# Elimination scratch in other buffers, more yields in it, and four HGRN tiles projected among the delta rule's pairs

## The chip, the cores and the metric

One core of a Trainium2 chip runs the whole kernel. The metric is the device time of one execution in microseconds (us). The kernel before was timed in three runs: median 3533.93 us, from 3527.35 to 3548.31.

## The reference

One decoder layer for 512 tokens of width 2048. Two groups of token mixers read the same normalised input through one projection `W_in`; a second part (PEER, an expert lookup) follows and is not touched.

```python
xn = rmsnorm(h)
a_q, a_f, a_i, a_g, b_q, b_k, b_v, b_z, b_b, b_a = split(xn @ w_in)
# HGRN2, 8 heads: S_t = diag(f_t) S_{t-1} + (1 - f_t) outer v_t;  o_t = S_t^T q_t
# gated delta rule, 8 value heads over 4 key heads, in chunks:
#   M = I + strict_lower(kb k^T * L);  u = M^-1 (v beta);  w = M^-1 (kb exp(gc))
#   v_new = u - w S;  o = (q exp(gc)) S + a_qk v_new;  S = S dl + kd^T v_new
h = h + concat(o_a, o_b) @ w_out
h = h + peer(rmsnorm(h))
```

## The kernel before

**The stream of projections.** `W_in` has 57 tiles of 128 columns. A tile is projected in 16 *steps*; a step (`mm3`) is three TensorE matmuls of 128x512 (high and low halves of weight and input), lines L239 to L241. A weight unit of eight steps is loaded by DMA (SP), its high half is cast on ACT (L100), and the low half is subtracted on POOL (L102); three buffers each. A finished tile gets a follow-up on DVE and ACT: a causal convolution and SiLU for q, k and v of the delta rule (`conv_silu`, L245, L362, L364, L369, tanh on ACT in L367), a gate (`gate`, L245, L285, tanh in L284), or f and K of an HGRN head (`forget`).

**The chains.** Beside that stream run the token mixers, one after the other: four pairs of delta rule heads (`gdn_pair`), then eight HGRN heads (`hgrn_head`). They are written as generators. `run` takes one piece of a chain, up to its `yield`, and then lets the stream go on by 1.8 steps on average in the pairs and by 5 in the HGRN heads. It stops the stream at a tile whose kind has two results waiting already (`self.live[self.coming] > 1`), since each kind has two buffers. `self.jobs()` is the order of the tiles.

**One pair.** Keys are normalised and multiplied (L420), the decays are applied on DVE (L432), and the diagonal 32x32 blocks go to DRAM and back (L435, L492), so that 32 blocks lie on 128 partitions. `substitute` then inverts them on DVE in 31 steps of a product (L498) and a sum (L500):

```python
for s in range(IB - 1):
    w = IB - 1 - s
    m = self.ft("t_sq", bufs=2)[:, 0:8 * IB].rearrange("p (j i) -> p j i", j=8)[:, :, 0:w]
    nc.vector.tensor_tensor(m, nb[...], T_[:, :, s:s + 1].to_broadcast([P, 8, w]), op=ALU.mult)
    nc.vector.tensor_tensor(T_[:, :, s + 1:], T_[:, :, s + 1:], m, op=ALU.add)
    if s % 4 == 3:
        yield
```

The product's buffer `t_sq` is also that of the squares for the norms (L376 on ACT, ahead of the norm's matmul L380). The result goes to DRAM and back (L504, L508), and TensorE combines the blocks to 64 and to 128 (`inverse`, L527 to L545; buffers `iTN` and `iY`, which nothing uses during the elimination). The q tile is normalised beside this (`unit_q`: L376, L380, ACT L151 and L152, DVE L383). Then each of the two heads runs a chain of small matmuls (L557 to L576) and a norm (L144, L145).

A scheduler orders the instructions of each engine ahead of time from the order in which they were written and from what each waits for; on the chip every engine takes its own in that order.

Of the kernel before, what the change touches and what calls it, by code (L numbers as in the profile page):

```python
# [33 lines left out]
IB = 32  # L34
# [43 lines left out]
class Kernel:  # L78
# [131 lines left out]
    def proj_steps(self, jobs):  # L210

        a, b = self.proj(jobs, 0), self.proj(jobs, 1)
        for _ in range(LAG):
            next(a)
            yield
        yield from self.zipped(a, b)
        for i in range(2, len(jobs)):
            yield from self.proj(jobs, i)
# [263 lines left out]
    def substitute(self):  # L482


        nc = self.nc
        TT = self.TT
        nb = self.ft("iN", (P, IB, IB))
        T_ = self.ft("iT", (P, 8, IB))
        nc.sync.dma_start(T_, self.a["eye"])
        yield  # L490
        for g in range(IG):
            nc.sync.dma_start(nb[g * NX:(g + 1) * NX], self.nd.rearrange("j h c s t -> (j h c) s t"))  # L492
        for _ in range(WAIT):
            yield
        for s in range(IB - 1):
            w = IB - 1 - s
            m = self.ft("t_sq", bufs=2)[:, 0:8 * IB].rearrange("p (j i) -> p j i", j=8)[:, :, 0:w]
            nc.vector.tensor_tensor(m, nb[:, s:s + 1, s + 1:].to_broadcast([P, 8, w]),  # L498
                                    T_[:, :, s:s + 1].to_broadcast([P, 8, w]), op=ALU.mult)
            nc.vector.tensor_tensor(T_[:, :, s + 1:], T_[:, :, s + 1:], m, op=ALU.add)  # L500
            if s % 4 == 3:
                yield
        for g in range(IG):
            nc.sync.dma_start(self.td.rearrange("j h c s t -> (j h c) s t")[:, 8 * g:8 * g + 8],  # L504
                              T_[g * NX:(g + 1) * NX])
        for j in range(P // IB):
            sl = slice(j * IB, (j + 1) * IB)
            nc.sync.dma_start(TT[sl, :, :, sl], self.td[j].rearrange("h c s t -> s h c t"))  # L508
        for _ in range(WAIT):
            yield  # L510
# [79 lines left out]
    def forget(self, ps, h):  # L590

        nc = self.nc
        th = self.ft("t_th", bufs=2)
        self.normed(th, ps)
        nc.scalar.activation(th, th, AF.Tanh, scale=0.5)
        F = self.ft("hF", bufs=2)
        nc.vector.tensor_scalar(F, th, self.f_mul[:, h:h + 1], self.f_add[:, h:h + 1], op0=ALU.mult, op1=ALU.add)
        K = self.ft("hK", bufs=2)
        nc.vector.tensor_scalar(K, th, self.k_mul[:, h:h + 1], self.f_mul[:, h:h + 1], op0=ALU.mult, op1=ALU.add)
        return F, K  # L600
# [121 lines left out]
    def jobs(self):  # L722

        key = lambda j: (36 + j, lambda ps: self.conv_silu(ps, 4 + j, "gk"), "k")
        out = [(56, self.gates, "gates")]
        for j in range(4):
            if j == 0:
                out.append(key(0))
            out.append((32 + j, lambda ps, j=j: self.conv_silu(ps, j, "gq"), "q"))
            for h in (2 * j, 2 * j + 1):  # L730
                if j < 3 and h % 2:
                    out.append(key(j + 1))
                out.append((40 + h, lambda ps, h=h: self.conv_silu(ps, 8 + h, "gv"), "v"))
                out.append((48 + h, self.gate, "u"))
        for h in range(8):
            out.append((8 + h, lambda ps, h=h: self.forget(ps, h), "f"))
            out.append((h, lambda ps: self.keep(ps, "hQ"), "r"))
            out.append((16 + h, lambda ps: self.keep(ps, "gv"), "v"))
            out.append((24 + h, self.gate, "u"))
        return out  # L740
# [605 lines left out]
```

## Time and profile before

| | |
|---|---|
| Median of three runs | 3533.93 us |
| The profiled execution | 3537.38 us |
| its span, first to last instruction | 3534.2 us |
| TensorE (PE) busy | 3323.9 us, 94% of the span |
| DVE busy | 2760.3 us, 78% |
| ACT busy | 1206.8 us, 34% |
| POOL busy | 878.8 us, 25% |
| Mean granted TensorE clock | 0.966 |

The first 1100 us or so hold the projections with the delta rule (from about 60 to 545 us), the HGRN heads and the output projection; PEER takes the rest. Busy shares are those of the whole span, and the change lies in its first sixth, so the stretches and waits of that part are what to read.

### The profile page before, as it was taken

To read this page: it belongs to the slowest core of one execution; us is meant where nothing else is said; L and a number is where in the kernel's file an instruction comes from. 1 tells how busy PE (TensorE), PEld (TensorE's weight loads), DVE (VectorE), ACT (ScalarE), POOL (GpSimd) and SP (SyncE) were. 2 spreads that over 40 slices of the span, in tenths; PEclk is the share of its full clock that TensorE was granted. 3 is DMA by queue.
4 is the path that set the end of the run, shared out by engine and by line. 5 is a ranking of instruction groups with operands and counts; after the bars stand their busy time and mean duration, and the time that the engine had idled before them with its cause. 6 is when DMAs were issued, how large, how long until landed. Compare 5 with 4: busy or idle time off the path is not lost.

```text
span 3534.2 us, 49832 instructions
## 1 busy us (share of the span) xinstructions
PE 3323.9 (94%) x19740; PEld 3085.3 (87%) x19740; DVE 2760.3 (78%) x4095; ACT 1206.8 (34%) x1499; POOL 878.8 (25%) x533
## 2 busy tenths in 40 slices
PE   7889899999999997898999799999999998999997
PEld 5667678888788896898989799999999998999997
DVE  7675654444534679998999799998999998999966
ACT  5333433322332212343435233332333334333334
POOL 4232223333354231011121222222222222111100
PEclk9899989999999998999999999999999999999999
DMA  4232222222442223677788899999999999999963
GB/s 147 76 96 88 83 64 81 78 81 78 130 130 85 71 66 120 209 293 292 277 318 294 316 346 375 370 368 355 358 360 365 372 366 333 349 322 335 332 183 111
DMA packets 238028, 801.63 MB, mean 227 GB/s; under 512 B 30202, under 2 KB 99066, under 8 KB 194978
## 3 DMA queue, kind: packets, MB, share of 16 engines
q1 hardware_dynamic: 191714, 462.88, 37.9%
q0 software_dynamic: 46080, 335.56, 25.2%
q8 instruction: 154, 2.52, 0.3%
q14 instruction: 80, 0.66, 0.1%
HBM read 754.50 MB, written 43.86 MB: 226 GB/s over the span
## 4 chain that ended last, share of the span: by engine, by line
PE 51%; DVE 19%; issue 14%; DMA 12%; POOL 2%; ACT 1%; SPq 0%; DVEq 0%; POOLq 0%; ACTq 0%
PE lin L239 8%; PE lin L241 7%; PE lin L240 7%; DMA row<-vn,eidx 3%; DVE wl L102 3%; DMA wr<-u 3%; PE g L1165 2%; PE g L1164 2%; PE g L1163 2%; POOL row L1205 2%; PE lin L1165 2%; PE lin L1164 2%; PE lin L1163 2%; DVE row L1218 2%; DMA wr<-v 1%
## 5 line engine op out<-in xcount | busy, mean ns | idle before, releaser
L100 ACT CAST wh<-wr 128x1024 fp32r<-128x1024 f32 x690 | 724.5, 1050 | 1708.8 <-DMA wr<-v 402.3
L241 PE MATMUL lin<-yh,wl 128*128 128x352 f32 x2048 | 673.0, 329 | 68.5 <-DVE wl L102 68.2
L102 DVE TENSOR_TENSOR wl<-wr,wh 128x1024 fp32r<-128x1024 f32 x512 | 623.3, 1219 | 81.6 <-ACT wh L100 80.3
L239 PE MATMUL lin<-yh,wh 128*128 128x352 f32 x2048 | 673.3, 329 | 9.5 <-ACT wh L100 9.5
L240 PE MATMUL lin<-yl,wh 128*128 128x352 f32 x2048 | 668.0, 326 | 0.0
L102 POOL TENSOR_TENSOR wl<-wr,wh 128x1024 fp32r<-128x1024 f32 x178 | 432.8, 2432 | 872.8 <-ACT wh L100 809.8
L241 PEld LDWEIGHTS lin<-yh,wl 128*128 128x128 f32 x2048 | 391.3, 191 | 78.8 <-DVE wl L102 78.4
L1205 POOL DMA_INDIRECT row<-un,eidx x160 | 212.4, 1328 | 809.7 <-DVE row L1218 626.2
L239 PEld LDWEIGHTS lin<-yh,wh 128*128 128x128 f32 x2048 | 391.7, 191 | 11.3 <-ACT wh L100 11.3
L1205 POOL DMA_INDIRECT row<-vn,eidx x160 | 201.2, 1258 | 782.8 <-DVE y_nat L1231 416.0
L240 PEld LDWEIGHTS lin<-yl,wh 128*128 128x128 f32 x2048 | 391.1, 191 | 0.0
L239 PE MATMUL lin<-xh,wh 128*128 128x512 f32 x912 | 381.4, 418 | 8.9 <-ACT xh L766 8.8
L1165 PE MATMUL g<-wgh,wl 128*128 128x352 f32 x1188 | 384.9, 324 | 3.5 <-DVE wl L102 3.3
L1164 PE MATMUL g<-wgl,wh 128*128 128x352 f32 x1188 | 385.4, 324 | 0.0
L1163 PE MATMUL g<-wgh,wh 128*128 128x352 f32 x1188 | 382.4, 322 | 2.3 <-ACT wh L100 2.3
L240 PE MATMUL lin<-xl,wh 128*128 128x512 f32 x912 | 375.5, 412 | 2.5 <-DVE xl L767 2.3
L241 PE MATMUL lin<-xh,wl 128*128 128x512 f32 x912 | 373.0, 409 | 4.4 <-POOL wl L102 4.4
L1231 DVE SCALAR_TENSOR_TENSOR y_nat<-row,ww,y_nat 128x2048 f32<-128x2048 f32 x128 | 300.3, 2346 | 11.1 <-DMA row<-vn,eidx 10.7
L1218 DVE SCALAR_TENSOR_TENSOR row<-row,hn_nat 128x2048 f32<-128x2048 f32 x128 | 292.1, 2284 | 1.7 <-DMA row<-un,eidx 1.5
L1165 PEld LDWEIGHTS g<-wgh,wl 128*128 128x128 f32 x1188 | 223.3, 188 | 5.5 <-DVE wl L102 5.4
L1163 PEld LDWEIGHTS g<-wgh,wh 128*128 128x128 f32 x1188 | 223.5, 188 | 2.6 <-ACT wh L100 2.6
L1164 PEld LDWEIGHTS g<-wgl,wh 128*128 128x128 f32 x1188 | 223.2, 188 | 0.0
(348 smaller groups left out, 5879.5 us busy)
## 6 DMA issues: line engine op xcount, KB each, us to landing
wr<-u SPq DMA_DIRECT2D x256, 512.0 KB, 6.2
wr<-v SPq DMA_DIRECT2D x256, 512.0 KB, 6.7
wr<-wi SPq DMA_DIRECT2D x114, 512.0 KB, 3.6
gd<-st SPq DMA_DIRECT2D x11, 2048.0 KB, 13.6
gm<-gd SPq DMA_DIRECT2D x32, 704.0 KB, 9.3
wr<-wo SPq DMA_DIRECT2D x32, 512.0 KB, 3.6
wr<-wq SPq DMA_DIRECT2D x32, 512.0 KB, 3.5
hidd<-hid SPq DMA_DIRECT2D x64, 176.0 KB, 5.2
```

The source lines that it names most:

```text
L100: nc.scalar.copy(hi, raw)
L102: (eng or nc.gpsimd).tensor_tensor(lo, raw, hi.bitcast(F32), op=ALU.subtract)
L239: mm(ps, hi, self.xh[:, k], start=first, stop=False)
L240: mm(ps, hi, self.xl[:, k], start=False, stop=False)
L241: mm(ps, lo, self.xh[:, k], start=False, stop=last)
L1163: nc.tensor.matmul(ps, hv[:, e, sl], wh[:, e], start=(e == 0), stop=False)
L1164: nc.tensor.matmul(ps, hv[:, e, sl], wl[:, e], start=False, stop=False)
L1165: nc.tensor.matmul(ps, lv[:, e, sl], wh[:, e], start=False, stop=(e == 3))
L1205: ins = nc.gpsimd.indirect_dma_start(out=r, out_offset=None, in_=self.a[tab], in_offset=bass.IndirectOffsetOnAxis(ap=idx, axis=0))
L1218: nc.vector.scalar_tensor_tensor(r, r, 1.0, hn, op0=ALU.mult, op1=ALU.mult, accum_out=ww[:, i:i + 1])
L1231: nc.vector.scalar_tensor_tensor(y, r, ww[:, i:i + 1], y, op0=ALU.mult, op1=ALU.add)
```

## The change

The products of the elimination alternate between `iTN` and `iY`; it yields after every second of its 31 steps instead of every fourth (15 times instead of 7); and `jobs` puts f and q of HGRN heads 0 and 1 behind the tiles of the four pairs, one each, where all of them stood behind the last pair.

```diff
         for s in range(IB - 1):
             w = IB - 1 - s
-            m = self.ft("t_sq", bufs=2)[:, 0:8 * IB].rearrange("p (j i) -> p j i", j=8)[:, :, 0:w]
+            m = self.ft(("iTN", "iY")[s % 2])[:, 0:8 * IB].rearrange("p (j i) -> p j i", j=8)[:, :, 0:w]
...
-            if s % 4 == 3:
+            if s % 2:
                 yield
...
     def jobs(self):
...
+        forget = lambda h: (8 + h, lambda ps: self.forget(ps, h), "f")
+        query = lambda h: (h, lambda ps: self.keep(ps, "hQ"), "r")
         out = [(56, self.gates, "gates")]
         for j in range(4):
...
+            out.append(forget(j // 2) if j % 2 == 0 else query(j // 2))
         for h in range(8):
-            out.append((8 + h, lambda ps, h=h: self.forget(ps, h), "f"))
-            out.append((h, lambda ps: self.keep(ps, "hQ"), "r"))
+            if h >= 2:
+                out += [forget(h), query(h)]
             out.append((16 + h, lambda ps: self.keep(ps, "gv"), "v"))
             out.append((24 + h, self.gate, "u"))
```

What this makes of the order is seen at two places, both in the second pair (pair 1). The first is ACT, from the convolution of a v tile (tanh in L367) on; `gq` is the pair's q tile, `wh` the cast weights, `t_th` a tanh. Before:

```order
L367 ACTIVATE t_th_1433<-t_y_1428 128x512
L100 CAST wh_1633<-wr_1631 128x1024
L100 CAST wh_1693<-wr_1691 128x1024
L284 ACTIVATE t_th_1526<-t_u_1527 128x512
L100 CAST wh_1763<-wr_1761 128x1024
L100 CAST wh_1857<-wr_1855 128x1024
L367 ACTIVATE t_th_1686<-t_y_1681 128x512
L100 CAST wh_1920<-wr_1918 128x1024
L376 ACTIVATE t_sq_1586<-gq_1289 128x512
L150 ACT_TABLE_LOAD
L151 ACTIVATE t_r_1626<-g_1624,epsc 128x512
L152 ACTIVATE t_r_1626<-t_r_1626 128x512
```

And now, from the square of q (L376) on:

```order
L376 ACTIVATE t_sq_1618<-gq_1361 128x512
L150 ACT_TABLE_LOAD
L100 CAST wh_1602<-wr_1600 128x1024
L367 ACT_TABLE_LOAD
L367 ACTIVATE t_th_1505<-t_y_1500 128x512
L100 CAST wh_1665<-wr_1663 128x1024
L100 CAST wh_1732<-wr_1730 128x1024
L284 ACTIVATE t_th_1588<-t_u_1589 128x512
L151 ACT_TABLE_LOAD
L151 ACTIVATE t_r_1646<-g_1644,epsc 128x512
L100 CAST wh_1791<-wr_1789 128x1024
L152 ACT_TABLE_LOAD
```

The square of q has moved from behind three tanh operations of the projections' follow-ups to ahead of all of them, and the root (L151, L152) now loads its table twice.

The second is DVE in the same pair's elimination, where the normalised q is written (L383). Before, near the elimination's end:

```order
L245 TENSOR_TENSOR pad_1842<-lin_1690,rstd_a 128x512
L498 TENSOR_TENSOR t_sq_1615<-iN_1419,iT_1420 128x8x6
L383 SCALAR_TENSOR_TENSOR gq_1289<-gq_1289,t_r_1626 128x512
L500 TENSOR_TENSOR iT_1420<-iT_1420,t_sq_1615 128x8x6
L362 TENSOR_SCALAR t_y_1845<-pad_1842,sm 128x512
L498 TENSOR_TENSOR t_sq_1618<-iN_1419,iT_1420 128x8x5
```

And now, after nine of its 31 products:

```order
L498 TENSOR_TENSOR iTN_1612<-iN_1481,iT_1482 128x8x23
L383 SCALAR_TENSOR_TENSOR gq_1361<-gq_1361,t_r_1646 128x512
L500 TENSOR_TENSOR iT_1482<-iT_1482,iTN_1612 128x8x23
L444 TENSOR_TENSOR geg_1414<-gq_1361,geg_1414 128x512
L498 TENSOR_TENSOR iY_1615<-iN_1481,iT_1482 128x8x22
L444 TENSOR_TENSOR geg_1428<-gq_1361,geg_1428 128x512
L500 TENSOR_TENSOR iT_1482<-iT_1482,iY_1615 128x8x22
```

The q work stands 17 products earlier; what surrounds it, one product and one sum in turn, is the same, with `iTN` and `iY` for `t_sq`. On TensorE the norm's matmul L380 follows 27, 34, 34 and 33.3 projection steps behind L420 in pairs 0 to 3, where 54.7, 51.7, 54 and 53.7 stood.

## Rows read from the trace of the kernel before

**Rows 1.** Windows: us; busy us of PE, PEld, DVE, ACT, POOL; clock; DMA.

```profile
100.00:200.00 100.00, 87.55 (x452) 67.42 (x451) 61.05 (x135) 37.93 (x56) 21.74 (x10) 0.83 0.25 76
600.00:700.00 100.00, 100.00 (x548) 83.82 (x548) 47.18 (x88) 27.38 (x32) 34.97 (x15) 1.00 0.26 80
```

**Rows 2.** Waits of TensorE, 60 to 560 us: who waited; total us, times, longest.

```profile
PE g L380 <- ACT t_sq L376: 30.2, 4, 9.1
PE g L527 <- DMA gT<-gTd: 6.5, 3, 3.1
PE g L145 <- DVE sql L121: 6.3, 6, 1.7
PE s L562 <- DVE gR L559: 4.3, 3, 1.6
```

**Rows 3.** Timeline of TensorE, pair 1: start, us, instruction, idle before and its end.

```profile
203.55 0.39 PE L239 MATMUL lin<-xh,wh 128*128 128x512 f32 x1
203.78 0.39 PE L240 MATMUL lin<-xl,wh 128*128 128x512 f32 x1
...
237.88 2.07 PE L380 MATMUL g<-t_sq,fc 128*128 128x512 f32 x2 [7.42 <-ACT t_sq L376]
...
257.80 0.60 PE L527 MATMUL g<-fc,gT 32*32 32x32 f32 x8 [3.11 <-DMA gT<-gTd]
```

**Rows 4.** Timeline of DVE: eliminations of pairs 1 and 2, L383 of pair 3.

```profile
213.68 0.40 DVE L498 TENSOR_TENSOR t_sq<-iN,iT 128x248 f32<-128x248 f32 x1
...
216.33 2.56 DVE L498 TENSOR_TENSOR t_sq<-iN,iT 128x224 f32<-128x224 f32 x1
...
239.99 0.23 DVE L498 TENSOR_TENSOR t_sq<-iN,iT 128x64 f32<-128x64 f32 x1 [0.58 <-PE g L380]
...
340.35 0.41 DVE L498 TENSOR_TENSOR t_sq<-iN,iT 128x248 f32<-128x248 f32 x1
...
371.71 0.18 DVE L500 TENSOR_TENSOR iT<-iT,t_sq 128x8 f32<-128x8 f32 x1
...
478.25 1.05 DVE L383 SCALAR_TENSOR_TENSOR gq<-gq,t_r 128x512 f32<-128x512 f32 x1 [2.26 <-ACT t_r L152]
```

**Rows 5.** Timeline of POOL in pair 1's elimination, first and last of four.

```profile
216.25 2.38 POOL L102 TENSOR_TENSOR wl<-wr,wh 128x1024 fp32r<-128x1024 f32 x1 [3.05 <-ACT wh L100]
...
242.49 2.73 POOL L102 TENSOR_TENSOR wl<-wr,wh 128x1024 fp32r<-128x1024 f32 x1 [8.67 <-ACT wh L100]
```

**Rows 6.** Timeline of SP: write and read of the blocks, pairs 1 and 3.

```profile
250.38 1.72 SPq L504 DMA_DIRECT2D gTd<-iT  x4
...
253.78 1.79 SPq L508 DMA_DIRECT2D gT<-gTd  x4
...
480.13 1.72 SPq L504 DMA_DIRECT2D gTd<-iT  x4
...
485.33 1.80 SPq L508 DMA_DIRECT2D gT<-gTd  x4
```

**Rows 7.** Waits of ACT, 60 to 560 us.

```profile
ACT t_th L367 <- DVE t_y L364: 61.0, 12, 10.0
```

**Rows 8.** Windows over the inverses of pairs 1, 2 and 3.

```profile
257.20:280.80 23.60, 23.00 (x151) 16.89 (x152) 3.24 (x11) 3.65 (x7) 2.36 (x1) 0.51 0.15 49
380.00:393.90 13.90, 13.90 (x149) 10.39 (x150) 8.74 (x18) 6.56 (x10) 2.36 (x1) 1.00 0.27 85
489.30:511.90 22.60, 22.60 (x151) 16.52 (x152) 3.24 (x11) 3.65 (x7) 3.21 (x2) 0.51 0.09 26
```

**Rows 9.** Timelines of TensorE and DVE, one level of HGRN head 0.

```profile
564.25 1.00 PE L624 MATMUL g<-hQ,hK 128*128 128x64 f32 x8
...
565.28 0.45 DVE L587 COPY_PREDICATED gL<-mk,g 128x256 f32<-128x256 uint8 x1 [2.19 <-PE g L624]
...
565.96 0.42 DVE L639 TENSOR_TENSOR hK<-hK,hf 128x256 f32<-128x256 f32 x1
```

**Rows 10.** Groups of instructions, 80 to 520 us: table loads of ACT.

```profile
L150 ACT ACT_TABLE_LOAD x13 | 16.7, 1283 | 0.2
```

## The prediction

> **What bounds the kernel now.** First two stretches of 100 us [rows 1]: from 100 to 200 us TensorE is busy 88 of 100 us and its clock is granted at 0.83 on average; from 600 to 700 us it is busy throughout, at 1.00. The order is the same from the middle of the second HGRN head on, so only what is lost before about 600 us can move. Then the waits of TensorE in that part [rows 2]: one line stands out, the norm of q (L380), 30.2 us in four waits, one in each pair, for the square on ACT (L376); behind it the first transpose of the inverse (L527), 6.5 us for the DMA of the eliminated blocks, and 10.6 us for norms (L145) and products (L562) in the heads' chains. Then pair 1 in order of time. A projection step is three matmuls at 0.227 us each, 0.68 us [rows 3]. TensorE runs steps until 230.5, stands 7.42 us, runs steps again until 254.7, stands 3.11 us and begins the inverse at 257.8 [rows 3].
>
> What ends that wait is on DVE. The elimination runs there from 213.68 [rows 4] until its write is issued at 250.38 [rows 6], without a break but two of 0.58 us, one of them at 239.99 [rows 4]; the read back is issued at 253.78 [rows 6]. So the path is elimination, write, read, inverse. TensorE's 7.42 us lie beside it: with the stop gone and nothing else changed, TensorE reaches L527 earlier and waits there instead. DVE is what holds the pair, and part of that is POOL: at 216.33 a product takes 2.56 us where the one at 213.68 takes 0.40 [rows 4], and POOL's weight subtraction has just begun at 216.25 [rows 5]. Each such halt costs 2.1 us. Pairs 0 to 3 have 5, 4, 3 and 4 of them in the elimination.
>
> **The change part by part.** No matmul, no vector operation and no DMA is added or removed; ACT gets five table loads more. All is order. What each moved piece costs:
>
> *The q norm.* L376 no longer shares a buffer with the elimination and is placed before it; L380 moves from behind 52 to 55 steps to behind 27 to 34. The 30.2 us go, but they are no term of the sum by themselves. The Trainium skill (Perfetto Trace Analysis, Optimization Strategy) takes the same gap repeating on the engine that should be full for a sign that buffers are short; by that rule the gap is closed with the buffer and the sum would be 30.2 us less (the first rival). The row that speaks against it is the end of DVE's work, which no buffer moves.
>
> *Steps inside the four stretches from L420 to L527.* The order holds 72.3, 72.7, 69.7 and 73.3 steps there before, and 72, 77.3, 75 and 70 now: 288.0 against 294.3. The stretch is ended by DVE, so a step in it is free, and it is one less later, where TensorE is full: 6.3 x 0.68 = **-4.3 us**. Twice the yields give no more than this, since the order already had its steps there and they now stand behind L380 instead of before it.
>
> *The length of the four stretches.* Pair 0: the same vector work; DVE's wait for L380 goes (0.7, where pair 1 has 0.58 at 239.99 [rows 4]), one more POOL halt: +1.4. Pair 1: the elimination stands behind the multiply of a gate tile (L285), whose projection now ends 28 steps after L420 instead of 21.3, so it begins 2.5 us later; half a halt more (1.0), waits of 1.2 gone: +2.3. Pair 2: it begins 3.3 us earlier (the k tile's convolution that stood before it moves in), but holds 4.3 us more of DVE work (that convolution, L383 and two L444) and 2.5 halts more (5.3), less 1.1 of waits and 1.5 at the write, which stood behind a weight load: +3.7 on the 31.5 us from 340.35 to 371.89 [rows 4]. Pair 3: begins 3.5 later (a v tile's projection ends after 23.3 steps, not 16.4), one more halt (2.1), 1.0 less work, the waits for L380 and for L383's factor gone (3.0, of it 2.26 in [rows 4]), and the read follows the write without a weight load between them, 5.2 us apart now against 3.4 in pair 1 [rows 6], 2.3 with what the landing gave back: -0.7. Sum **+6.7 us**. The halts are the unknown: TensorE no longer stops, so it draws weights faster and POOL works more within the elimination. Nine subtractions belong to each stretch; I count those whose cast ACT can reach, for ACT stands in order behind tanh operations that wait for DVE, 61.0 us in twelve waits already [rows 7]. If as many fall in as before, the sum of the four is -3.8; if two more than I count in each, +23.5.
>
> *The head's chain.* It gets 10, 7 and 15 steps more in pairs 0 to 2. TensorE is full there but for the 10.6 us of short waits [rows 2], so the steps only move; I take half of the waits as filled: **-5.3 us** (none to -10.6).
>
> *The clock in the inverse.* The stretch from L527 to L442 ran 13.9 us at a clock of 1.00 in pair 2, and 22.6 and 23.6 at 0.51 in pairs 3 and 1 [rows 8]; 1.00 is 2.4 GHz, 0.50 is 1.2. Pair 2 is the one without a wait at L527 ahead of it; the other three are the waits of [rows 2]. Now pair 2 waits there too: the longest stop at L380, 9.1 us, was its own, less 3.6 for the 5.3 steps more, plus 3.7 for the longer stretch, is 9.2 us. Then its inverse goes as pair 3's: 22.6 - 13.9 = **+8.7 us** (0 if the clock stays).
>
> *Heads 0 and 1 of HGRN.* Head 0 begins at projection step 513 instead of 474.3, and the next f tile may not be projected until head 0 frees a buffer, so the order puts 2 steps between levels there, ten times, where 5 stood. A level needs 1.03 us from its matmuls to the masked copy and 1.10 on DVE [rows 9], 2.2 with the hand-over; two steps and the eight matmuls are 2.2. So the levels are just even, and a POOL halt or a tile's follow-up work shows; the norm and the state chain with 2 and 0.33 steps beside them wait some 1.5 and 1.2 us. **+5 us**, between 0 and 15 (ten levels with a halt's 2.1 at every second one, and the rest).
>
> *The table loads.* 1.28 us each on ACT [rows 10], which is busy 38 us of 100 [rows 1]; they lie between L151 and L152, long before L383 is due. Nothing; if DVE waited for each, 6 us.
>
> Sum: 6.7 - 4.3 - 5.3 + 8.7 + 5 = +10.8 us. The profiled execution took 3537.4 us, 3.2 of it around its span, and so 3548.2; the median shown is 3533.9, 0.1% lower, and against that it is **3545 us**, +0.3%. What a measurement of this kernel can tell from no change is about 0.5%, 17.7 us, so the forecast is no difference: one stall dissolves and comes back as another.
>
> **The rivals.** *The stall was the bound.* If DVE's elimination ends about 7 us earlier in every pair, TensorE does not wait at L527, 30.2 us go: 3504 us; the inverses at full clock would come on top. For it: 30.2 us is the largest wait in this part [rows 2], and while TensorE stood, ACT stood too. Against: DVE had only 1.2 us of idle in pair 1's elimination, and TensorE still waited 3.11 us after it in [rows 3]. Chance 0.14.
>
> *POOL takes the elimination's time.* One mechanism, in one place: with TensorE running on, all nine subtractions of a stretch could fall into the elimination but those before its start, seven instead of the five I count on average. Two halts more in each pair at 2.1 us are 17 us: 3562. It decides when the casts do not stay behind ACT's tanh. For it: pair 0 has five already, and the gaps in POOL's row are the times when TensorE or ACT stood [rows 5]. Against: the tanh waits remain. Beside it, the Trainium skill (Perfetto Trace Analysis, Optimizing Scalar/DVE Operations) has the two engines share an SBUF port and doubts that moving work between them helps; the trace agrees, 2.56 us against 0.40. Chance 0.18.
>
> *The fill is missing later.* 39 steps are spent early; if heads 0 and 1 stall at every level, 15 us instead of 5, and the chain's waits stay: 3560. For it, the 2 steps in ten places; against, that 2.2 us stand against 2.2. Chance 0.10.
>
> That the change does not do what it says can be left aside: the four tiles are projected before head 0 (step 513 against 474.3), and the products do go to other buffers. Twice the yields, though, hardly add steps to the elimination, and that is in the forecast.
>
> **How the numbers follow.** Forecast within 0.5% (3516 to 3552): 0.58. Slower by more: POOL 0.18 and the heads 0.10, together 0.28. Faster by more: 0.14. The lower ends of the terms (-3.8 - 4.3 - 10.6, clock and heads 0) give -19, that is 3515; the upper ones of the two likelier unknowns (heads 15, chain 0, eight halts more) give +43, of which I take two thirds, since they need not come together: 3563. The range is 3512 to 3563: it reaches a little into the first rival, and leaves out 0.1 on either side.
>
> **What would show it.** In the changed profile L380 no longer waits, and L527 waits in all four pairs, 9 to 10 us each, for the same DMA. The eliminations take 33 to 40 us, with 4 to 6 halts each. The inverse of pair 2 runs at half clock. Heads 0 and 1 show idle time on TensorE, a few us. Wrong it is if L527's waits sum to less than 15 us, if the inverses run at 1.00, or if the idle before 560 us falls by over 20 us.

## The result, and the profile after

The changed kernel takes 3553.78 us (median of six runs, 3547.17 to 3567.63) against 3533.56 for the kernel before in as many: a ratio of 1.0064, interval 1.0037 to 1.0092. The forecast was 3545 and "no difference". The time lies in the range, 9 us above the forecast, and the ratio just beyond the half per cent that was set as a difference. The profiled executions stand 14.5 us apart, 3551.85 against 3537.38. Head 2 of HGRN starts 15.7 us later (654.83 against 639.16), and from there to the end the two profiles stay some 9 to 20 us apart: the loss lies where the prediction looked.

The waits of TensorE from 60 to 620 us in the changed kernel (who waited, for whom; total us, times, longest), which answer to [rows 2], and below them the two stretches of [rows 1]:

```profile
PE g L527 <- DMA gT<-gTd: 48.0, 4, 13.4
PE g L145 <- DVE sql L121: 5.0, 5, 1.8
PE g L159 <- DVE t_y L325: 3.6, 1, 3.6
PE s L562 <- DVE gR L559: 2.7, 2, 1.7
```

```profile
100.00:200.00 100.00, 86.98 (x462) 68.22 (x461) 58.63 (x129) 34.92 (x49) 24.49 (x10) 0.83 0.26 78
600.00:700.00 100.00, 98.23 (x565) 81.18 (x566) 48.77 (x102) 28.87 (x35) 30.35 (x14) 1.00 0.24 74
```

L380 waits no more; its 30.2 us and the 6.5 of L527 have become 48.0 us at L527. Pair 2 in order of time, TensorE and then DVE's elimination:

```profile
384.25 0.39 PE L241 MATMUL lin<-xh,wl 128*128 128x512 f32 x1
395.89 0.58 PE L527 MATMUL g<-fc,gT 32*32 32x32 f32 x8 [11.25 <-DMA gT<-gTd]
```

```profile
350.09 0.42 DVE L498 TENSOR_TENSOR iTN<-iN,iT 128x248 f32<-128x248 f32 x1 [1.20 <-DMA iN<-gNd]
...
350.99 0.41 DVE L498 TENSOR_TENSOR iY<-iN,iT 128x240 f32<-128x240 f32 x1
351.43 2.61 DVE L500 TENSOR_TENSOR iT<-iT,iY 128x240 f32<-128x240 f32 x1
...
389.38 0.17 DVE L500 TENSOR_TENSOR iT<-iT,iTN 128x8 f32<-128x8 f32 x1
```

TensorE stops for 11.25 us behind L241; the elimination, in which DVE has no break of over 0.1 us, ends at 389.55, 39.5 us after it began, and the write and the read back follow. The 2.61 us sum beside a 0.42 us product is a halt: POOL's subtraction begins at 351.38.

The windows over the four inverses, L527 to L442 (us; busy PE, PEld, DVE, ACT, POOL; clock; DMA), which answer to [rows 8]:

```profile
135.08:158.08 23.00, 23.00 (x151) 16.89 (x152) 5.93 (x12) 6.85 (x10) 3.52 (x2) 0.50 0.10 30
266.15:289.18 23.03, 23.03 (x151) 16.92 (x152) 3.24 (x11) 4.94 (x8) 2.35 (x1) 0.50 0.13 34
395.89:418.89 23.00, 23.00 (x151) 16.89 (x152) 6.20 (x12) 4.29 (x8) 2.35 (x1) 0.50 0.11 29
524.15:547.18 23.03, 23.03 (x151) 17.04 (x152) 3.24 (x11) 3.66 (x7) 2.37 (x1) 0.50 0.17 49
```

Pair 2's inverse, the one at 1.00 before, has fallen to half clock with the others.

### The profile page after: what moved, and what is told of

It is laid out like the page before. It is cut to its first block, busy times and chain, and to the rows that moved or that the text cites. A ratio compares the mean times of both kernels' runs of the same rounds, so it can differ in the third digit from the quotient of the medians.

```text
span 3549.9 us, 49836 instructions
## 1 busy us (share of the span) xinstructions
PE 3327.9 (94%) x19740; PEld 3091.3 (87%) x19740; DVE 2771.6 (78%) x4095; ACT 1213.7 (34%) x1504; POOL 878.6 (25%) x533
## 4 chain that ended last, share of the span: by engine, by line
PE 45%; DVE 23%; issue 16%; DMA 12%; POOL 2%; ACT 1%; SPq 0%; DVEq 0%; POOLq 0%; ACTq 0%
PE lin L239 7%; PE lin L241 7%; PE lin L240 6%; DVE wl L102 4%; DMA wr<-u 3%; DVE row L1222 3%; POOL row L1209 2%; DMA wr<-v 2%; DMA row<-vn,eidx 2%; PE g L1169 2%; PE g L1168 2%; PE g L1167 2%; DVE hT L1170 2%; DVE iT L500 2%; PE lin L115 1%
## 5 line engine op out<-in xcount | busy, mean ns | idle before, releaser
L241 PE MATMUL lin<-yh,wl 128*128 128x352 f32 x2048 | 673.7, 329 | 68.7 <-DVE wl L102 68.6
L241 PEld LDWEIGHTS lin<-yh,wl 128*128 128x128 f32 x2048 | 392.0, 191 | 78.8 <-DVE wl L102 78.7
L241 PE MATMUL lin<-xh,wl 128*128 128x512 f32 x912 | 372.4, 409 | 4.5 <-POOL wl L102 4.5
```

The costliest lines, as they stand in the source:

```text
L241: mm(ps, lo, self.xh[:, k], start=False, stop=last)
```

## The experiments

Theory: the pair is held by the elimination and its way through DRAM; a stall of TensorE beside it is free, and moved ahead of the inverse it costs clock. The table gives for each run the ratio to the kernel before on the same chip, and from its profile TensorE's idle time at L380 and L527 (lines of the changed kernel; in others they are some lines further down), the summed length of the four inverses, and when head 2 of HGRN starts. That start comes from one profiled execution, but nothing of PEER stands ahead of it. In each run the median differs from that of the kernel before by 2 to 10 us more than head 2 does.

| run | median us | ratio, interval | idle us | inverses us | head 2 us |
|---|---|---|---|---|---|
| before | 3533.6 | 1 | 36.7 | 81.8 | 639.2 |
| the change | 3553.8 | 1.0064 (1.0037 to 1.0092) | 48.0 | 92.1 | 654.8 |
| e1_buffers | 3554.8 | 1.0059 (1.0043 to 1.0076) | 52.3 | 89.0 | 651.3 |
| e2_yields | 3552.4 | 1.0045 (1.0033 to 1.0058) | 45.3 | 88.4 | 652.2 |
| e3_jobs | 3534.5 | 0.9990 (0.9977 to 1.0004) | 36.5 | 73.4 | 629.8 |
| e4_buf_yield | 3556.3 | 1.0059 (1.0036 to 1.0083) | 54.2 | 91.7 | 654.5 |
| e5_warm104 | 3563.6 | 1.0085 (1.0064 to 1.0106) | 0 | 61.2 | 657.7 |
| e6_fill18 | 3528.5 | 0.9980 (0.9955 to 1.0005) | 20.5 | 86.4 | 628.2 |
| e7_dve | 3553.0 | 1.0055 (1.0033 to 1.0078) | 48.8 | 91.1 | 653.4 |
| e8_fill18_dve | 3529.6 | 0.9982 (0.9959 to 1.0004) | 17.9 | 85.0 | 624.4 |
| e9_fill_warm | 3509.9 | 0.9942 (0.9919 to 0.9965) | 0 | 50.1 | 612.6 |
| e10_fill_warm_oldbuf | 3530.4 | 1.0009 (0.9987 to 1.0031) | 16.2 | 50.1 | 631.6 |

### Which part of the change costs

**Buffers alone** (the kernel before with this one line):

```diff
-            m = self.ft("t_sq", bufs=2)...
+            m = self.ft(("iTN", "iY")[s % 2])...
```

> Only the products' buffers are changed; yields and the order of the projections are those of the kernel before. Theory (TensorE's stall at the q norm was off the path; it comes back at L527, and the clock pays for where it stands): no idle time before L380 in 60 to 560 us (before 30.2), 8 to 13 us before L527 in every pair (before 6.5 in all), eliminations of about their old lengths (32 to 38 us), and pair 2's inverse at 0.51 instead of 1.00, 23 us long instead of 14.4: +8.6 against the kernel before, about 3542 beside its 3533.6. Rival 1 (the stall was the bound): the idle time goes without coming back, about 3504. Rival 2 (the loss comes from the yields or from the four tiles): no difference, 3534, and pair 2's inverse stays at 1.00.

Waits of TensorE, 60 to 560 us, and the window of pair 2's inverse:

```profile
PE g L527 <- DMA gT<-gTd: 52.3, 4, 16.0
```

```profile
387.13:407.00 19.87, 19.87 (x159) 14.47 (x160) 4.44 (x12) 5.57 (x9) 2.36 (x1) 0.70 0.19 60
```

By the medians the line that removes the stall makes the whole loss, and at head 2 it makes 12.1 of the 15.7 us. The stall came back with more than it was, in waits of 10.7 to 16.0 us, and pair 2's inverse lost its clock, to 0.70 and not 0.51 as expected; its cost, +5.5 us, is under the 8.6, and the kernel is 19.6 us slower (12.1 at head 2) where 8.6 were expected. What the expectation left out is in the section on why.

**Yields alone**, and **jobs alone**:

```diff
-            if s % 4 == 3:
+            if s % 2:
```

> Only the yields are doubled; buffers and order of the projections are those of the kernel before. Theory: the products still share their buffers with the q norm's square, so the idle time before L380 stays, 15 to 35 us in all; some 16 steps more stand before the heads, each worth 0.68 us there and back; four or five halts of 2.1 us in each elimination; about 3534 to 3544, the upper end if pair 2's inverse falls to half clock. Rival (the halts of the steps pulled in are the loss of the whole change): eliminations longer by 2 us or more each and 3545 or above with pair 2's inverse at 1.00.

> Only the order of the projections is changed: the two forget gates and two queries of heads 0 and 1 stand among the pairs'. Theory: about as many steps run in the pairs as before (the stream isn't held up for a free buffer sooner than before), so the same work in another order: 3530 to 3538, idle time before L380 stays, 20 to 35 us. Rival (the four tiles cost the time, by their tanh and their DVE work in the elimination or by other table loads): 3545 or above.

Waits of TensorE, 60 to 560 us, and the window of pair 2's inverse with the yields alone, and the inverses of pairs 2 and 3 with the jobs alone:

```profile
PE g L527 <- DMA gT<-gTd: 26.9, 4, 9.4
PE g L380 <- ACT t_sq L376: 18.4, 4, 4.8
```

```profile
396.01:415.36 19.35, 19.35 (x159) 14.23 (x160) 3.74 (x11) 5.57 (x9) 2.37 (x1) 0.73 0.14 51
```

```profile
373.85:388.32 14.47, 14.47 (x158) 11.13 (x159) 4.80 (x15) 5.46 (x9) 2.37 (x1) 1.00 0.22 79
484.63:499.54 14.91, 14.91 (x160) 11.24 (x160) 7.00 (x15) 4.29 (x8) 3.44 (x2) 1.00 0.23 72
```

The yields do by half what the buffers do: the stop at L380 shrinks to 18.4 us, L527's grows to 26.9, pair 2's inverse falls to 0.73. The 3552.4 us are above the 3544 expected. Its four eliminations hold 22 subtractions of POOL where the kernel before has 17, and are 11.5 us longer in sum, so the rival has a share in it; but it asked for a pair 2 at 1.00, and that did not hold. The jobs cost nothing. There the wait at L527 was missing in pair 3 too, and its inverse took 14.9 us where pair 3's took 22.6 [rows 8]: head 2 starts 9.4 us earlier. The median shows none of that, and why the rest of that program gives it back stays open.

**Buffers and yields, old jobs:**

> Buffers and yields of the change, the order of the projections as before. Theory (the four tiles cost nothing of their own, as alone): the changed kernel's time, 3548 to 3558, with 11 to 14 us idle before L527 and half clock in every inverse. Rival (without the four tiles the stream is held up for a buffer sooner, so fewer steps fill pair 3): more idle time in pair 3, 3560 or above.

As expected, but for a wait of 16.0 us at L527 in pair 1, where 11 to 14 were expected: the parts do not add up, they are two ways of moving the same wait.

### Is it the hole ahead of the inverse?

**Added matmuls.** In the changed kernel, right before L527:

```diff
+        wps = self.pt("g")
+        for _ in range(104):
+            nc.tensor.matmul(wps, self.xh[:, 0, 0:P], self.xh[:, 0], start=True, stop=True)
```

> The changed kernel with 104 matmuls of 128x512 on constant operands before each pair's L527, whose result nothing reads; nothing else is changed. They take 104 x 0.215 = 22.4 us on TensorE, where the changed kernel has 11 to 13 us of idle time and some 15 steps (10 us) that the order then puts behind them. Theory (half clock in the inverse comes from the idle time before it, and is what the change lost): idle before L527 under 2 us in every pair, granted clock of the inverses 0.95 to 1.00, 14 to 16 us long instead of 22 to 23, so 4 x 8 = 32 us less than the changed kernel, about 3520, below the kernel before too. Rival 1 (the inverse's own small matmuls bring the clock down): inverses stay at 0.51 to 0.6 and 22 us, time 3550 to 3560. Rival 2 (the path of a pair runs over VectorE and the DMAs, and the inverse is not on it): clock at 1.00, yet 3545 or above.

The group of the added matmuls (60 to 560 us; busy us, mean ns, idle before) and the inverse of pair 0:

```profile
L513 PE MATMUL g<-xh 128*128 128x512 f32 x416 | 94.9, 389 | 0.0
```

```profile
137.89:154.00 16.11, 16.11 (x166) 12.45 (x166) 7.70 (x14) 4.11 (x8) 2.59 (x1) 1.00 0.11 35
```

All four inverses ran at 1.00, 12.4 to 16.3 us long, with 12.3 steps inside them in pairs 0 to 2 instead of 7.3. So the theory on the clock held, and rival 1 fell. The time did not: the kernel became 9.8 us slower than the changed one. The expectation had forgotten that the steps which the order put behind the added matmuls still have to run. 94.9 us were added where 48.0 were idle: 46.9 us more work for 9.8 us more time by the medians, and 2.9 us at head 2. So some 37 to 44 us did come back; the inverses are 30.9 us shorter and hold 14 steps more. Filling a hole with nothing pays only its clock. The second rival, that the inverse is not on the path, had forecast just this, full clock and 3545 or above. This run alone leaves it standing; the run with both, below, speaks against it, for there the inverses at 1.00 bring time.

**Real steps in the hole.** In the changed kernel, with the rate set back to 1.0 at the next pair's keys:

```diff
-        for _ in range(WAIT):
+        for _ in range(WAIT + 18):
             yield
...
         yield from self.substitute()
+        self.pace = 0.45
...
-            owed = min(owed + rate, OWED)
+            owed = min(owed + rate * self.pace, OWED)
```

> The changed kernel, but 18 more yields between a pair's elimination and its inverse, and the rate of steps cut to 0.45 from there to the next pair's key products: 88, 87 and 90 projection steps now stand ahead of L527 in pairs 0 to 2 (before 72, 78 and 75), the chains lose as many, and pair 3 has no free buffers for more (69). Theory (the time is lost as idle time before L527 and as half clock behind it, and real work in the hole wins both back): idle before L527 under 4 us in pairs 0 to 2, about 11 in pair 3; inverses of pairs 0 to 2 at 0.95 to 1.00 and 13 to 16 us long; 3 x (8 to 11 idle + 8 clock) = 48 to 57 less than the changed kernel, less some 6 for longer stretches: 3500 to 3515, below the kernel before too. Rival 1 (a pair is VectorE's and the DMAs' path, and the pulled-in steps lengthen the elimination by their halts and evacuations as much as they fill): the idle time stays over 6 us and the time 3540 or above. Rival 2 (what the chains lose comes back as idle time in them): chains idle by 10 us or more each, 3535 to 3550.

Waits from 60 to 560 us (L529 is the change's L527), TensorE ahead of pair 0's inverse, and the windows of the inverses of pairs 0 and 3:

```profile
PE g L529 <- DMA gT<-gTd: 20.5, 3, 14.1
```

```profile
134.37 0.40 PE L240 MATMUL lin<-xl,wh 128*128 128x512 f32 x1
136.47 0.49 PE L241 MATMUL lin<-xh,wl 128*128 128x512 f32 x1 [1.71 <-POOL wl L102]
136.90 0.40 PE L529 MATMUL g<-fc,gT 32*32 32x32 f32 x8
```

```profile
136.90:157.89 20.99, 20.99 (x149) 15.72 (x149) 3.32 (x12) 2.61 (x6) 4.60 (x2) 0.52 0.24 77
501.50:524.50 23.00, 23.00 (x151) 16.89 (x152) 3.25 (x11) 3.66 (x7) 2.36 (x1) 0.50 0.11 37
```

25 us less than the changed kernel by the medians (26.7 at head 2), and no longer slower than the kernel before, but 3528.5 us where 3500 to 3515 were expected: the idle time went as expected in pairs 0 and 1 (0 and 1.9 us at L527; 4.6 in pair 2, over the 4 expected), but the clock did not come back, and the four eliminations sum to 158.0 us, 8.5 more than in the changed kernel. Pair 0 spoke against the theory: no wait at L527, and half clock all the same. The row shows a stop of 1.71 us one matmul earlier, for POOL's weight half.

**Both together**: in the kernel with the 18 yields, added matmuls right before L527 of each pair, 14, 16, 28 and 130 of them. This tells whether a stop or the small matmuls themselves bring the clock down:

```diff
+        warm = self.pt("g")
+        for _ in range((14, 16, 28, 130)[j]):
+            nc.tensor.matmul(warm, self.xh[:, 0, 0:P], self.xh[:, 0], start=True, stop=True)
```

> The kernel of run e6_fill18 with 14, 16, 28 and 130 matmuls of 128x512 on constant operands right before L527 of pairs 0, 1, 2 and 3 (3.0, 3.4, 6.0 and 28 us; in pair 3 the order puts some 20 steps behind them that stood ahead). Theory (idle time right ahead of an inverse brings it to half clock, so what real steps leave of the hole has to be filled too): no idle time before L527, inverses at 1.00 and 12 to 16 us instead of 21.0, 21.0, 21.4 and 22.8: 30 us gained, 6 us of the added matmuls beyond the holes lost, 3500 to 3510, about 30 below the kernel before. Rival 1 (the inverse's own small matmuls bring the clock down, with or without a hole, since e6_fill18's pair 0 ran at half clock with no idle time before L527): inverses stay at 0.50 to 0.55 in pairs 0 to 2, 3528 to 3540. Rival 2 (pair 0 alone stays at half clock, as its 1.7 us of idle time stands before the last step, ahead of the added matmuls): 3507 to 3517.

TensorE ahead of pair 0's inverse and the four windows:

```profile
137.37 0.51 PE L241 MATMUL lin<-xh,wl 128*128 128x512 f32 x1 [1.72 <-POOL wl L102]
137.71 3.36 PE L520 MATMUL g<-xh 128*128 128x512 f32 x14
```

```profile
141.00:153.42 12.42, 12.42 (x149) 9.45 (x149) 3.17 (x11) 2.61 (x6) 1.45 (x1) 1.00 0.27 87
254.83:267.69 12.86, 12.86 (x152) 9.81 (x152) 4.97 (x11) 3.66 (x7) 2.64 (x2) 1.00 0.39 133
369.79:382.20 12.41, 12.41 (x150) 9.44 (x150) 6.24 (x10) 4.29 (x8) 2.37 (x1) 1.00 0.50 174
485.24:497.65 12.41, 12.41 (x150) 9.44 (x150) 3.17 (x11) 2.61 (x6) 0.00 (x0) 1.00 0.01 2
```

The same stop of 1.7 us stands in pair 0, but 14 large matmuls lie between it and the small ones, and the clock stays at 1.00. So the small matmuls do not bring it down by themselves, and they do not bring it back either: the same 149 matmuls of pair 0 took 12.4 us from 1.00 on, and 21.0 at 0.52 in the run before. The kernel takes 3509.85 us, 0.58% under the kernel before (interval 0.35 to 0.81) and some 44 us under the changed one, at the upper edge of what was expected. It beats both.

**The old buffers in that kernel:**

> Run e9_fill_warm with one thing undone: the products are in the buffers that they share with the q norm's square, as in the kernel before. Theory (removing TensorE's stall pays once the time that it frees is filled, and only then): the stall before L380 is back with 15 to 30 us in all, and now adds to the path in pairs 0 to 2, 10 to 25 us over e9_fill_warm. Rival (the stall is off the path whatever TensorE does, and the buffers never mattered): no more than 5 us over it.

Waits of TensorE, 60 to 560 us:

```profile
PE g L380 <- ACT t_sq L376: 16.2, 4, 4.6
```

20.5 us slower by the medians, 15.9 by the spans (3525.2 against 3509.3) and 18.9 at head 2, for 16.2 us of waiting at L380. The stall that was worth nothing, and whose removal cost 12 us at head 2 and 20 by the medians, is worth about all of its length once the time it frees is used.

### POOL's halts

> The changed kernel with the weight halves that are emitted during an elimination subtracted on VectorE (1.2 us each) instead of GpSimd, three in each elimination. Theory (GpSimd's subtraction holds an elimination's operation up by about 2.1 us): two or three halts fewer in each, the eliminations 2 to 4 us shorter (33 to 37 us), L527's idle time 2 to 4 us less in each pair, inverses still at half clock: 3540 to 3548, 6 to 14 under the changed kernel. Rival (the halts only show up; the elimination waits as long for something else): no difference, 3550 to 3558. A third way: VectorE's queue waits there for a weight's copy, and the eliminations get longer: 3560 or above.

> The 18 yields and the subtraction on VectorE together. Theory: as the run with the 18 yields alone, and 2 to 4 us less in each of the stretches whose L527 still waits: 3490 to 3510. Rival: VectorE's queue waits for a weight's copy and gives it back: no less than with the yields alone.

Neither moved the time beyond its interval; head 2 starts 1.5 us earlier than in the changed kernel, and 3.8 earlier than with the 18 yields alone. The run did not do what it was meant to: the order put the 13 subtractions that went to VectorE mostly outside the eliminations, POOL still had 5, 6, 5 and 5 inside them (6, 5, 6 and 5 in the changed kernel), and VectorE's own take 1.2 us each. The eliminations sum to 151.1 us against 149.5. What the halts are worth was not measured.

## Why the prediction was right or wrong

The reason was right: the 30.2 us are beside the path, and come back at L527. The terms, against the two profiles (a step taken at its 0.68 us):

| term | predicted us | measured us |
|---|---|---|
| length of the four stretches | +6.7 | +3.9 |
| steps in them | -4.3 | -4.3 (6.3 more) |
| the heads' chains, pair to pair | -5.3 | -0.6 |
| clock in the inverses | +8.7 | +10.3 |
| pair 3's inverse to head 0 | none | +3.7 |
| heads 0 and 1 | +5 | +2.4 |

These make 15.4 us; with 1.7 steps fewer inside the inverses (+1.1) and pair 0's keys 0.8 earlier it is the 15.7 us of head 2. That the forecast of 10.8 us comes within 5 us of this is in part luck: the chains and the stretch that it left out cost 8.4 us more than it had, and the length of the stretches and the heads 5.4 less.

- *The stretches.* Pair by pair -0.5, +3.5, +2.8 and -1.9 for +1.4, +2.3, +3.7 and -0.7. The eliminations took 37.5, 38.2, 39.5 and 34.4 us with 6, 5, 6 and 5 subtractions of POOL in them: inside "33 to 40 us, with 4 to 6 halts". The second rival, seven in each, did not come. That a halt is POOL's doing is read from the two starts beside each other, and no run took the subtractions away; it agrees with the Trainium skill (SBUF — State Buffer, section on its two separate sides, on the port pair that DVE and GpSimd share), which has the later of the two wait for the whole instruction: 2.61 us here beside 0.42.
- *The chains.* This is the step that failed, "I take half of the waits as filled". The three chains from an inverse to the next pair's keys, before and then now (us; busy TensorE; clock; DMA):

```profile
158.09:194.29 36.20, 32.30 (x174) 0.97 0.31 100
280.83:319.12 38.29, 34.65 (x186) 0.99 0.25 83
393.92:426.76 32.84, 29.91 (x168) 1.00 0.28 89
```

```profile
158.09:199.16 41.07, 39.31 (x202) 0.96 0.32 103
289.18:332.68 43.50, 39.79 (x207) 0.98 0.28 94
418.89:463.51 44.62, 41.60 (x217) 0.98 0.27 88
```

  They got 33 steps more and grew by 21.9 us, 33 x 0.68 = 22.4. TensorE's idle time in them fell from 10.5 to 8.5 us, in the first of them alone, and half clock in them, now all of it right behind the inverses, took 2.0 us more of the busy time than before. Together that is nothing, and it alone is 5 of the missing microseconds. Another 4 lie in a stretch the sum did not have, from pair 3's inverse to head 0: 28.9 us before, 31.7 now with 1.3 steps less, 2.3 us of it new idle time.
- *The wait at L527* was to be 9 to 10 us in each pair and is 11.3, 13.4, 11.3 and 12.1. The four waits should have summed to 30.2 + 6.5 + 6.7 - 4.3 = 39.1, or 36.3 with the measured +3.9; they are 48.0. The missing 9 to 12 us are a second thing that the old stall did. Windows of the kernel before around its stop in pair 3 (456 to 463.2 us steps, then the stop, then what ran behind it):

```profile
456.00:463.20 7.20, 7.20 (x33) 5.71 (x31) 6.92 (x9) 2.55 (x3) 4.83 (x2) 1.00 0.22 73
463.20:470.00 6.80, 0.10 (x1) 0.00 (x0) 6.18 (x22) 1.12 (x2) 0.00 (x0) 0.70 0.23 77
470.00:476.00 6.00, 5.92 (x12) 4.02 (x13) 5.08 (x23) 2.78 (x4) 0.00 (x0) 0.50 0.01 3
```

  The stop at L380 itself took the clock to half, and it stayed there for 3 to 6 us of the steps behind. 12 matmuls ran in those 6 us. Over the four stretches the half clock cost TensorE's busy time 2.9, 2.4, 2.7 and 3.1 us, 11.1 in all, and nothing in the changed kernel. Without the stop these steps run at full clock and TensorE is early at L527 by that much more. In the stretches this is free, as all else there; it only makes the hole larger.
- *The clock.* Right in mechanism and size: pair 2's inverse went from 14.4 to 23.0 us (the forecast's 13.9 starts half a microsecond behind L527), and pairs 0 and 3 add 1.7. What the old stall also did is now plain: it ended 14 to 20 us ahead of the inverse, with steps in between in which the clock recovered; the new one stands right before the small matmuls.
- *The first rival*, the stall as the bound, fell with the result. The Trainium skill's rule (Perfetto Trace Analysis, Optimization Strategy) that a gap repeating on the engine that should be full can mean too few buffers named the cause of the gap rightly; that closing it brings its time is what no run showed until the hole behind it was filled too.
- *The third rival*, heads 0 and 1 starving: short waits of 0.7 to 1.1 us at L624 and L631 did appear, 2.8 us idle in all where there were 1.5, and the heads cost less than forecast. The 39 steps of this rival are 36: 513 is counted to L624 of head 0, 474.3 to L614, and at L614 it is 510.7 now.

The range held the time. The half per cent did not quite: by medians the difference is 20.2 us, above the 17.7 that stood for no difference, though the interval of the ratio reaches down to 1.0037.

## What to carry to other kernels

Before a stall is removed, follow what ends the stretch it stands in: if another engine or a transfer does, the stall reappears there, and the question is what stands behind it in the new place. Here that was a run of small matmuls that paid with half clock. Such a removal is half a change; the other half is to bring real work into the time it frees, and with both the kernel was faster than before either.

## What had not been expected of the hardware

- A stop right ahead of a run of small matmuls costs more than its length: after 1.71 us of idle time the next 21 us ran at 0.52, with TensorE busy throughout, where they take 12.4 us at 1.00 (pair 0 of the runs with the 18 yields, without and with the added matmuls). After stops of 7 to 9 us ahead of large matmuls the clock was back at 1.00 within 3 to 6 us.
- In the twelve profiles the 15 inverses at 1.00 have no idle time of over 0.1 us right ahead of them, but for one with 1.0 us; the other 33 have 1.4 us or more, at L527 or, in pair 0 of the two runs with 18 yields and no added matmuls, one matmul earlier. The Trainium skill (TensorE: Matmul & The Clock Gate, section on HAM oscillation) describes a kernel in which a wait for a DMA precedes each short piece of matmul work, and each piece starts at half clock; the windows above agree.
- The clock can be bought: 188 added matmuls of 128x512, 43.3 us in all and 22.8 of it beyond the idle time they filled, brought head 2 of the kernel with the 18 yields 15.5 us forward; by the medians it is 18.7 us, and 13.8 when each is taken against the kernel before on its own chip.
- Two inverses were at 0.70 and 0.73 on average, behind waits of 16.0 and 5.7 us, where others behind 5 to 16 us stayed at 0.50 to 0.56. The length of the wait does not tell them apart; what runs inside them does. In both, ten matmuls of 128x512 stand in a row between the small ones, from 7.3 us on, and the clock is back at 1.00 towards their end. The other 31 below 1.00 have at most seven in a row. No run varied this alone. The inverse of pair 2 with the buffers alone, ahead of the ten, over them and behind:

```profile
387.13:394.46 7.33, 7.33 (x57) 4.87 (x57) 0.13 (x1) 2.63 (x4) 0.00 (x0) 0.50 0.29 89
394.46:398.98 4.52, 4.52 (x13) 3.15 (x11) 0.56 (x1) 0.73 (x2) 0.00 (x0) 0.51 0.00 0
398.98:407.00 8.02, 8.02 (x94) 6.45 (x94) 3.75 (x11) 2.21 (x3) 2.36 (x1) 1.00 0.20 66
```
